# A decoder block on one core: constants loaded later, mixing moved a unit on, gates paired by branch, head outputs turned among the last row blocks

## The chip, the core and the metric

The kernel runs on one core of a Trainium2 chip. The metric is the device time of one execution in microseconds (us). An execution's time holds the span that the profile shows and what lies around it. TensorE (PE) multiplies matrices, VectorE (DVE) and ScalarE (ACT) work on elements, GpSimd (POOL) does small jobs, and SyncE (SP) issues most of the DMA transfers. Each engine works through its own list of instructions in order, and semaphores tell it when an operand is there.

## The reference

One layer of a decoder block in float32, on 1024 positions of width 1024. The parts that matter here:

```python
u = rms_norm(h, mix_pre_g)
z = jnp.einsum('bsd,de->bse', u, w_in)
p, q, k, v = z[..., :o1], z[..., o1:o2], z[..., o2:o3], z[..., o3:o4]
gate_a, gate_b = z[..., o4:o5], z[..., o5:]
ya = jnp.einsum('bsc,cd->bsd', pool_mixer(p, pool_mix, pool_scale), w_branch_a)
yb = jnp.einsum('bsc,cd->bsd', diff_attention(q, k, v, ...), w_branch_b)
m = jax.nn.sigmoid(gate_a) * ya + jax.nn.sigmoid(gate_b) * yb
h = h + rms_norm(jnp.einsum('bsd,de->bse', m, w_out), mix_post_g)
# then a SwiGLU FFN of 2816 hidden columns
```

The pooling mixer takes running means over windows of 2, 4, 8 and 16 positions, one window for each of four groups of 128 channels, subtracts the input, mixes each group by a 128x128 matrix (`pool_mix`) and scales the channels (`pool_scale`). Differential attention has four heads. A head computes two softmaxes over causal scores with a linear bias, and uses the first minus lambda times the second; lambda comes from four vectors of 64 (`lam_q1` to `lam_k2`). Each head's output rows are normed and scaled by `subln_g` and a constant.

## The kernel before

Every operand of a matmul is split into a rounded part (`_hi`) and a residual (`_lo`), and a product is three matmuls: hi x hi, lo x hi, hi x lo. ScalarE writes most rounded parts, VectorE subtracts them from the source for the residuals.

**Projection.** Two columns blocks of 128 of `w_in`, with all 1024 positions, form a unit. A unit (`unit`, which calls `seven_steps`) computes its 2x2 blocks by seven products of 12 matmuls each in place of eight, on sums of the input's quadrants (A11 to A22, S1 to S4, made by `half_sums` on VectorE) and of the weights' quadrants (T1 to T4, made in `weights`). `done` takes each finished block (e is the column block, t the half of the positions) to where it goes. The first two heads' q and k are computed without that scheme while the input is still being normed and turned, by the functions `first_pair` and `common`; their blocks are stored by `qk_done` (L312 is the residual of q). Then come units for heads 2 and 3, four units for v and the pooled channels (`vp_unit`; `pool` takes the running means and mixes), and eight units for the gates, the unit d holding column block d of both gates. `gate_done` applies the sigmoid on ScalarE (L571) and stores the block in DRAM (`sgd`). What `pool` has to do is put in a list, `later`, and done at the start of the next unit's code, behind the loading of its weights.

**Constants.** Pool scale (`psc`), the gain of the head norm (`sgc`) and the four lambda vectors (`lamt`, whose tile shows as sg in the profile) are cleared on POOL (L472) and loaded by SyncE (L587 to L590); VectorE reduces the vectors (L593), ScalarE scales the gain (L600). The order on each engine is not that of the source: a scheduler hoists instructions whose operands it holds to be ready, and so this group stands between the half sums of the input, ahead of head 1's last blocks.

**Attention.** A row block of 128 queries goes through `scores` (matmuls, L690 and L691; VectorE adds the bias and takes the row extreme, L694; ScalarE takes the exponential, L697), `transposes` (L718, with ScalarE and VectorE copies) and `values` (L732; then ScalarE L737, VectorE L738, and ScalarE's square sum for the norm, L128). `seq` lists the row blocks: head after head, in the order QORDER within each. Scores run four row blocks ahead of values. Between the steps a filler gives TensorE other matmuls, some for each step as PACES says: the end of the last gate unit, and then the first branch (`branch` with e = 0: pooled outputs times `w_branch_a`, times the gate loaded from `sgd`, into `ma`). After a head's last row block `head_norm` takes the norm on POOL (L124), and four steps later (LAG) VectorE scales the head's rows (L748).

**After attention.** All four heads' outputs `O` are turned, 32 transposes of 128x128 on TensorE into PSUM tiles oT (L810); ScalarE writes the rounded part OTh (L812), VectorE the residual OTl (L813). Then the second branch (e = 1) computes column blocks 0 to 7 for both halves of the positions, adds the first branch's, and the output projection and the FFN follow.

SBUF tiles come from two rings, `a8` (16 tiles of 8 KB a partition) and `b4` (14 of 4 KB); PSUM has two banks for each of `mm` and `fil` and two tiles of two banks, `pair`. A tile can be written only when the last reader of its place in the ring is through.

Of the kernel before, what the change touches and what calls it, by code (L numbers as in the profile page):

```python
# [11 lines left out]
F32R = mybir.dt.float32r  # L12
# [3 lines left out]
P = 128  # L16
# [16 lines left out]
QORDER = (7, 0, 6, 1, 5, 2, 4, 3)  # L33
LAG = 4
# [5 lines left out]
def block_kernel(ctx, tc, x, w_in, pool_mix, pool_scale, w_branch_a, lam_q1, lam_k1, lam_q2,  # L40
# [121 lines left out]
    def split(o, a):  # L162
        hi, lo = o
        nc.scalar.copy(hi, a)  # L164
        sub(lo, a, hi)
        return o
# [245 lines left out]
    with tc.manual_schedule(engines={nc.tensor.engine, nc.scalar.engine, nc.vector.engine, nc.gpsimd.engine}):  # L412
# [58 lines left out]
        for t in (psc, sgc, lamt):  # L471
            nc.gpsimd.memset(t, 0.0)  # L472
# [64 lines left out]
    def pool(g, p, s0):  # L537
# [17 lines left out]
        split(y, p)  # L555
        o = pair("y")
# [10 lines left out]
    def gate_done(d):  # L567
        st, seen = [b4([P, S], F32, "g_st") for _ in range(2)], [0, 0]

        def done(e, t, src):  # L570
            nc.scalar.activation(st[e][:, half(t)], src, AF.Sigmoid)  # L571
# [59 lines left out]
    for d in range(KD - 1):  # L631
        if d == 3:
            next(head0)
        unit(w_cols(o_ga, d), w_cols(o_gb, d), gate_done(d))

    last_unit = seven_steps(weights(w_cols(o_ga, KD - 1), w_cols(o_gb, KD - 1)), U, gate_done(KD - 1))
# [16 lines left out]
    def branch(e, w, mov, take):  # L653

        for d in range(KD):
            bh, bl = load_w(w[:, d * P:(d + 1) * P], 4, P, "wb", e == 0)
            for t in range(2):
                sg = temp(("p1", "sg")[t])
                nc.sync.dma_start(sg, sgd[e][d][:, half(t)])
                o = fil("branch")  # L660
                for k in range(4):
                    triple(o, bh[:, k, :], bl[:, k, :], *mov(t, k), k == 0, k == 3, False)
                    yield
                take(d, t, o, sg)
# [78 lines left out]
    def head_norm(h):  # L743
        r = rstd_of(oss[h], NB, P)
        defer(LAG, lambda: scale_head(h, r))

    def scale_head(h, r):
        nc.vector.tensor_tensor(out=O[h], in0=O[h], in1=r.unsqueeze(2).to_broadcast([P, NB, P]), op=ALU.mult)  # L748
# [15 lines left out]
    seq = [(h, qb) for h in range(NH) for qb in QORDER]  # L764
# [18 lines left out]
    for i in range(-AHEAD, len(seq)):  # L783
# [21 lines left out]
    OT = [(a8([P, 2, S], F32R, "OTh"), a8([P, 2, S], F32R, "OTl")) for _ in range(2)]  # L805
    for h in range(NH):
        for t in range(2):
            pt = mm("oT")
            for i in range(4):
                nc.tensor.transpose(pt[:, i * P:(i + 1) * P], O[h][:, t * 4 + i, :], ident)  # L810
            dh, dl = OT[h // 2][0][:, h % 2, half(t)], OT[h // 2][1][:, h % 2, half(t)]
            nc.scalar.mul(dh, pt, sgc)  # L812
            nc.vector.scalar_tensor_tensor(out=dl, in0=pt, scalar=sgc, in1=f32(dh), op0=ALU.mult,  # L813
                                           op1=ALU.subtract)

# [404 lines left out]
```

## Time and profile before

| | us |
|---|---|
| median of three runs | 1288.24 |
| fastest and slowest of the three | 1286.24, 1288.36 |
| profiled execution | 1285.73 |
| its span | 1283.9 |
| PE busy in the span | 1254.4 |
| DVE, ACT, POOL busy | 835.6, 583.3, 142.7 |

The span goes from the first to the last instruction of one execution; 1.8 us of that execution lie around it. Busy is the time in which an engine worked on at least one instruction. A row of the timeline gives start, duration, engine, line and operation, what is written and read, and in brackets how long the engine stood idle before it and what ended that. In the projection TensorE starts a matmul of 512 columns every 0.227 us. The projection takes the span up to about 350 us, attention goes from there to about 500, the second branch to 545, and the output projection and the FFN take the rest.

### The profile page before, as it was taken

The numbers are of one execution on the slowest core, as the hardware profiler recorded it, in microseconds if no ns is written. First come the engines' busy times: TensorE is split into PE (matmuls) and PEld (weight loads), VectorE is DVE, ScalarE is ACT, GpSimd is POOL, SyncE is SP. The second block draws the span as 40 slices with busy tenths as digits, with TensorE's granted clock in tenths as the row PEclk, the third lists the DMA queues.
The fourth block names the chain that finished last, engine by engine and source line by source line (L and its number), as shares of the span: only waits on it lengthen the run. The fifth ranks groups of instructions, "written<-read, shape, count | busy, mean of one in ns | idle before, by whom it ended". The sixth has DMA issues, their size and how long they took to land.

```text
span 1283.9 us, 15774 instructions
## 1 busy us (share of the span) xinstructions
PE 1254.4 (98%) x5912; PEld 1041.6 (81%) x5912; DVE 835.6 (65%) x1297; ACT 583.3 (45%) x1037; POOL 142.7 (11%) x131
## 2 busy tenths in 40 slices
PE   8899999999989998999999999999999999999997
PEld 8788778888778887878878888888888888888886
DVE  5785766345479997665599565556556537965666
ACT  7453344434586675244454333333333333554542
POOL 4100000000101100001102110111110111000221
PEclk9899999999999999999999999999999999999999
DMA  8254336233688412544224223233223268833235
GB/s 255 94 164 164 136 133 217 82 131 107 210 264 220 135 52 65 184 146 163 83 90 140 88 85 115 99 107 123 99 100 98 95 197 279 266 107 94 88 106 205
DMA packets 139788, 179.16 MB, mean 140 GB/s; under 512 B 8000, under 2 KB 94528, under 8 KB 137280
## 3 DMA queue, kind: packets, MB, share of 16 engines
q1 hardware_dynamic: 129024, 146.70, 36.5%
q10 hardware_dynamic: 10688, 31.46, 6.4%
q8 instruction: 46, 0.75, 0.3%
q14 instruction: 30, 0.25, 0.1%
HBM read 124.39 MB, written 53.74 MB: 139 GB/s over the span
## 4 chain that ended last, share of the span: by engine, by line
PE 81%; DVE 7%; DMA 4%; ACT 3%; issue 2%; POOL 2%; SPq 0%; ACTq 0%; DVEq 0%; POOLq 0%
PE Y L231 9%; PE Y L232 9%; PE Y L233 9%; PE X L231 5%; PE X L232 5%; PE X L233 5%; PE Yd L232 3%; PE Yd L233 3%; PE Yd L231 3%; PE Z L232 2%; PE Z L233 2%; PE Z L231 2%; PE o L732 2%; PE wo L873 2%; PE wo L874 2%
## 5 line engine op out<-in xcount | busy, mean ns | idle before, releaser
L160 DVE TENSOR_TENSOR p<-Z,p 128x512 f32<-128x512 f32 x35 | 24.2, 691 | 159.2 <-PE Z L233 155.6
L232 PE MATMUL Y<-A_lo,Wh 128*128 128x512 f32 x296 | 115.6, 391 | 0.3 <-DVE A_lo L87 0.3
L231 PE MATMUL Y<-A_hi,Wh 128*128 128x512 f32 x296 | 115.3, 390 | 0.0
L233 PE MATMUL Y<-A_hi,Wl 128*128 128x512 f32 x296 | 115.2, 389 | 0.0
L231 PE MATMUL Y<-S_hi,Wh 128*128 128x512 f32 x280 | 109.2, 390 | 0.0
L232 PE MATMUL Y<-S_lo,Wh 128*128 128x512 f32 x280 | 109.2, 390 | 0.0
L231 PE MATMUL X<-S_hi,Wh 128*128 128x512 f32 x280 | 109.1, 389 | 0.1
L233 PE MATMUL Y<-S_hi,Wl 128*128 128x512 f32 x280 | 109.1, 390 | 0.0
L233 PE MATMUL X<-S_hi,Wl 128*128 128x512 f32 x280 | 109.0, 389 | 0.0
L232 PE MATMUL X<-S_lo,Wh 128*128 128x512 f32 x280 | 109.0, 389 | 0.0
L200 ACT CAST Wh<-wf_t 128x1024 fp32r<-128x1024 f32 x70 | 72.8, 1053 | 71.8 <-PE X L232 30.6
L200 ACT CAST Wh<-w_raw 128x1024 fp32r<-128x1024 f32 x72 | 60.6, 843 | 65.6 <-PE Z L232 40.0
L87 DVE TENSOR_TENSOR w_op<-wd,w_op 128x512 fp32r<-128x512 f32 x77 | 56.3, 732 | 51.0 <-ACT w_op L164 51.0
L87 DVE TENSOR_TENSOR Wl<-wf_t,Wh 128x1024 fp32r<-128x1024 f32 x70 | 86.6, 1244 | 2.9 <-ACT Wh L200 2.9
L164 ACT CAST w_op<-wd 128x512 fp32r<-128x512 f32 x77 | 47.9, 622 | 74.6 <-PE Yd L233 31.3
L87 DVE TENSOR_TENSOR Wl<-w_raw,Wh 128x1024 fp32r<-128x1024 f32 x72 | 69.5, 966 | 14.0 <-ACT Wh L200 14.0
L232 PE MATMUL Yd<-w_op,s_op 128*128 128x512 f32 x176 | 68.7, 390 | 0.3 <-DVE w_op L87 0.2
L231 PE MATMUL Yd<-w_op,s_op 128*128 128x512 f32 x176 | 68.6, 390 | 0.0
L233 PE MATMUL Yd<-w_op,s_op 128*128 128x512 f32 x176 | 68.3, 389 | 0.0
L160 DVE TENSOR_TENSOR wf_t<-w_raw,wf_t 128x512 f32<-128x512 f32 x70 | 65.7, 938 | 1.0
L232 PEld LDWEIGHTS Y<-A_lo,Wh 128*128 128x128 f32 x296 | 55.6, 188 | 12.1 <-DVE A_lo L87 0.7
L231 PEld LDWEIGHTS Y<-A_hi,Wh 128*128 128x128 f32 x296 | 55.6, 188 | 11.5
(266 smaller groups left out, 3062.3 us busy)
## 6 DMA issues: line engine op xcount, KB each, us to landing
s_raw<-fsd SPq DMA_DIRECT2D x35, 512.0 KB, 3.6
w_raw<-in_w_in_dram SPq DMA_DIRECT2D x32, 512.0 KB, 4.2
w_raw<-in_w_ffn_gate_dram SPq DMA_DIRECT2D x22, 512.0 KB, 3.8
w_raw<-in_w_ffn_up_dram SPq DMA_DIRECT2D x22, 512.0 KB, 3.8
fsd<-fss SPq DMA_DIRECT2D x11, 1024.0 KB, 3.9
wd<-in_w_ffn_down_dram SPq DMA_DIRECT2D x44, 256.0 KB, 5.4
fsd<-F SPq DMA_DIRECT2D x33, 256.0 KB, 2.3
qkd<-qk_st ACTq DMA_DIRECT2D x16, 512.0 KB, 3.8
```

The costliest lines, as they stand in the source:

```text
L87: nc.vector.tensor_tensor(out=o, in0=a, in1=f32(hi), op=ALU.subtract)
L160: nc.vector.tensor_tensor(out=o, in0=a, in1=b, op=op)
L164: nc.scalar.copy(hi, a)
L200: nc.scalar.copy(hi, a)
L231: nc.tensor.matmul(o, ah, bh, start=start, stop=False, skip_group_check=goes_on)
L232: nc.tensor.matmul(o, ah, bl, start=False, stop=False, skip_group_check=goes_on)
L233: nc.tensor.matmul(o, al, bh, start=False, stop=stop, skip_group_check=goes_on)
L732: nc.tensor.matmul(o, ats[b // 4][:, j, b % 4 * P:(b % 4 + 1) * P], V[:, b, :, :], start=b == 0 and j == 0, stop=b == qb and j == 1)
L873: nc.tensor.matmul(o[e], mh[:, k, :], wl, start=False, stop=False)
L874: nc.tensor.matmul(o[e], ml[:, k, :], wh, start=False, stop=k == KD - 1)
```

## The change

Four things are changed.

1. The constants' tiles are cleared later: no longer by memsets after the first heads, but at head 3, by POOL copies that read head 2's q tile (the values are overwritten by the loads). The loads cannot come before.
2. `pool` ends with the split of its result; the mixing is a function of its own, `mix`, put in `later` for the unit after. `unit` does only what was in the list when it began.
3. The gate units hold two column blocks of the same gate: first gate a's blocks in pairs, then gate b's. Of the last pair, gate b's blocks 6 and 7, which are finished among the attention's first steps, the values are stored as they are, and the second branch applies the sigmoid when it has loaded them.
4. The last head's row blocks run from 7 to 0. Heads 0 to 2 are turned after its rows 7, 6 and 5 (`turn_head`, in a PSUM tile of `pair`), the upper half of head 3 is normed after row 4, the lower after row 0, and each is turned some steps later. The second branch takes the upper halves of column blocks 0 and 1 first.

```diff
+QLAST = (7, 6, 5, 4, 3, 2, 1, 0)
...
-        for t in (psc, sgc, lamt):
-            nc.gpsimd.memset(t, 0.0)
...
         split(y, p)
+        later.append(lambda: mix(g, pm, y))
+
+    def mix(g, pm, y):
         o = pair("y")
...
+    GATES = [(e, d) for e in range(2) for d in range(KD)]
+    gate_pairs = [GATES[i:i + 2] for i in range(0, 2 * KD, 2)]
+    unfinished = gate_pairs[-1]
...
-            nc.scalar.activation(st[e][:, half(t)], src, AF.Sigmoid)
+            if pair == unfinished:
+                nc.scalar.copy(st[e][:, half(t)], src)
+            else:
+                nc.scalar.activation(st[e][:, half(t)], src, AF.Sigmoid)
             seen[e] += 1
             if seen[e] == 2:
-                nc.scalar.dma_start(sgd[e][d], st[e])
+                b, d = pair[e]
+                nc.scalar.dma_start(sgd[b][d], st[e])
...
-        while later:
+        for _ in range(len(later)):
             later.pop(0)()
...
     for h in range(2, NH):
-        unit(w_cols(o_q, h), w_cols(o_k, h),
-             W=W if h == 2 else None, done=partial(qk_done, h, st=[a8([P, 2, S], F32R, "qk_st") for _ in range(2)]))
-
+        st = [a8([P, 2, S], F32R, "qk_st") for _ in range(2)]
+        if h == 3:
+
+            for t in (psc, sgc, lamt.rearrange("p i d -> p (i d)")):
+                nc.gpsimd.tensor_copy(t, f32(late[:, 0, :t.shape[-1]]))
+        late = st[0]
+        unit(w_cols(o_q, h), w_cols(o_k, h), W=W if h == 2 else None, done=partial(qk_done, h, st=st))
...
+        order = [(d, t) for d in range(KD) for t in range(2)]
+        if e == 1:
+            order[:4] = [(0, 1), (1, 1), (0, 0), (1, 0)]
...
+            if (e, d) in unfinished:
+                nc.scalar.activation(sg, sg, AF.Sigmoid)
...
+    def turn_head(h, t):
+
+        if len(OT) <= h // 2:
+            OT.append((a8([P, 2, S], F32R, "OTh"), a8([P, 2, S], F32R, "OTl")))
+        pt = pair("oT")[:, 0, :]
+        for i in range(4):
+            nc.tensor.transpose(pt[:, i * P:(i + 1) * P], O[h][:, t * 4 + i, :], ident)
+        dh, dl = OT[h // 2][0][:, h % 2, half(t)], OT[h // 2][1][:, h % 2, half(t)]
+        nc.scalar.mul(dh, pt, sgc)
+        nc.vector.scalar_tensor_tensor(out=dl, in0=pt, scalar=sgc, in1=f32(dh), op0=ALU.mult, op1=ALU.subtract)
...
-    seq = [(h, qb) for h in range(NH) for qb in QORDER]
+    seq = [(h, qb) for h in range(NH) for qb in (QLAST if h == NH - 1 else QORDER)]
...
-            if (i + 1) % len(QORDER) == 0:
-                head_norm(i // len(QORDER))
+            h, pos = divmod(i, len(QORDER))
+            if h < NH - 1 and pos == len(QORDER) - 1:
+                head_norm(h)
+            elif h == NH - 1 and pos < NH - 1:
+                for t in range(2):
+                    turn_head(pos, t)
+            elif h == NH - 1 and pos % 4 == 3:
+                b = slice(4, 8) if pos == 3 else slice(0, 4)
+                head_norm(h, b)
+                defer(LAG, partial(turn_head, h, b.start // 4))
...
-    for h in range(NH):
-        for t in range(2):
-            pt = mm("oT")
```

How this moves instructions on the engines is shown at three places. First VectorE, before, where the sums of the input's last quadrants end the first stage (A_raw and S_raw hold the sums, A_lo the residuals, sg_153 the lambda vectors, lsum their products' sums, qk_st head 1's q and k):

```order
L160 TENSOR_TENSOR S_raw_93<-S_raw_93,S_raw_94 128x4x128
L593 ISA sg_153,lsum_1054<-sg_153 128x64
L593 ISA lsum_1054 128x1
L160 TENSOR_TENSOR A_raw_91<-S_raw_93,A_raw_91 128x4x128
L160 TENSOR_TENSOR S_raw_94<-S_raw_94,A_raw_91 128x4x128
L160 TENSOR_TENSOR A_raw_92<-A_raw_92,A_raw_91 128x4x128
L312 SCALAR_TENSOR_TENSOR qk_st_575<-q_154,qk_st_575 128x512
L87 TENSOR_TENSOR qk_st_578<-k_155,qk_st_578 128x512
```

Of the change, the place where the same reduction (now L611) stands, in the unit of head 2 (p_141 and u_142 take its blocks, Y_801 and X_803 are its products; Wl and wf_t are weights of the unit behind head 3):

```order
L161 TENSOR_TENSOR p_141_830<-Y_801,p_141_830 128x512
L611 ISA sg_153,lsum_1054<-sg_153 128x64
L611 ISA lsum_1054 128x1
L88 TENSOR_TENSOR Wl_1079<-w_raw_1074,Wh_1078 128x1024
L88 TENSOR_TENSOR qk_st_800<-p_141_830,qk_st_800 128x512
L161 TENSOR_TENSOR u_142_844<-X_803,u_142_844 128x512
L611 ISA sg_153,lsum_1054<-sg_153 128x64
L611 ISA lsum_1054 128x1
L88 TENSOR_TENSOR Wl_1087<-wf_t_1082,Wh_1086 128x1024
```

The first reduction moved from between the sums of the first stage to some 40 rows later on VectorE; the three sums now follow each other directly.

Second, ScalarE at the start of attention, before (E is a row block's scores, nm their row extremes, g_st a gate's blocks, AT the transposed weights of attention):

```order
L697 ACT_TABLE_LOAD
L697 ACTIVATE E_2743,sums_2746<-E_2743,nm_2745 128x1024
L697 ACTIVATE E_2744,sums_2746<-E_2744,nm_2745 128x1024
L571 ACT_TABLE_LOAD
L571 ACTIVATE g_st_2706<-p_464_2754 128x512
L697 ACT_TABLE_LOAD
L697 ACTIVATE E_2788,sums_2790<-E_2788,nm_2789 128x128 x2
L697 ACTIVATE E_2831,sums_2834<-E_2831,nm_2833 128x896
L571 ACT_TABLE_LOAD
L571 ACTIVATE g_st_2707<-p_468_2780 128x512
L697 ACT_TABLE_LOAD
L697 ACTIVATE E_2832,sums_2834<-E_2832,nm_2833 128x896
```

The same place of the change:

```order
L722 ACT_TABLE_LOAD
L722 ACTIVATE E_2743,sums_2746<-E_2743,nm_2745 128x1024
L722 ACTIVATE E_2744,sums_2746<-E_2744,nm_2745 128x1024
L582 COPY g_st_2706<-p_464_2754 128x512
L722 ACTIVATE E_2788,sums_2790<-E_2788,nm_2789 128x128 x2
L722 ACTIVATE E_2831,sums_2834<-E_2831,nm_2833 128x896
L582 COPY g_st_2707<-p_468_2780 128x512
L722 ACTIVATE E_2832,sums_2834<-E_2832,nm_2833 128x896
L582 COPY g_st_2707<-u_474_2807 128x512
```

The sigmoids became copies, and the table loads between them and the exponentials are gone, but for the first.

Third, TensorE at the end of attention, before (o is a row block's output before the norm, O the outputs of heads 0 to 3 as O_2735 to O_2738, branch the second branch's sums):

```order
L718 MATMUL aT_4535<-ident,E_4427 128x128 x4
L732 MATMUL o_4543<-V_3720,AT_4514 128x256 x8
L732 MATMUL o_4543<-V_3720,AT_4519 128x256 x2
L732 MATMUL o_4564<-V_3720,AT_4540 128x256 x8
L810 MATMUL oT_4641<-ident,O_2735 128x128 x4
L810 MATMUL oT_4648<-ident,O_2735 128x128 x4
L231 MATMUL branch_4705<-OTh_4637,wb_hi_4698 128x512
L810 MATMUL oT_4655<-ident,O_2736 128x128 x4
L232 MATMUL branch_4705<-OTl_4638,wb_hi_4698 128x512
```

Of the change, the turning of head 1 among the scores of the last head (branch is still the first branch, the filler):

```order
L715 MATMUL s_4371<-K_3710,QA_3709 128x384
L716 MATMUL s_4371<-K_3710,QB_3719 128x384
L232 MATMUL branch_4657<-y2h_2982,wb_hi_4650 128x512
L789 MATMUL oT_4419<-ident,O_2736 128x128 x4
L233 MATMUL branch_4657<-y2l_2983,wb_hi_4650 128x512
L234 MATMUL branch_4657<-y2h_2982,wb_lo_4651 128x512
L232 MATMUL branch_4657<-y2h_2982,wb_hi_4650 128x512
L789 MATMUL oT_4426<-ident,O_2736 128x128 x4
L233 MATMUL branch_4657<-y2l_2983,wb_hi_4650 128x512
L757 MATMUL o_4401<-V_3720,AT_4309 128x256 x8
```

and the last row blocks of the change, with the filler's last matmuls and the first of the second branch:

```order
L232 MATMUL branch_4673<-y2h_2982,wb_hi_4650 128x512
L789 MATMUL oT_4591<-ident,O_2738 128x128 x4
L757 MATMUL o_4598<-V_3720,AT_4567 128x256 x6
L743 MATMUL aT_4615<-ident,E_4512 128x128
L233 MATMUL branch_4673<-y2l_2983,wb_hi_4650 128x512
L234 MATMUL branch_4673<-y2h_2982,wb_lo_4651 128x512
L232 MATMUL branch_4710<-OTh_4347,wb_hi_4703 128x512
L233 MATMUL branch_4710<-OTl_4348,wb_hi_4703 128x512
L234 MATMUL branch_4710<-OTh_4347,wb_lo_4704 128x512
L757 MATMUL o_4620<-V_3720,AT_4588 128x256 x4
L757 MATMUL o_4628<-V_3720,AT_4617 128x256 x2
```

Of the eight turns, six moved up among the last head's row blocks and one stands among its last; the one left, of head 3's lower half, comes 16 matmuls of the second branch behind the last row block. The filler ends among the last row blocks instead of ahead of them.

More of the change, by code (lines that the diff above doesn't have):

```diff
@@ L630, in block_kernel @@
     head0 = load_head(0)
-    for d in range(KD - 1):
-        if d == 3:
+    for i, pair_cols in enumerate(gate_pairs[:-1]):
+        if i == 3:
             next(head0)
-        unit(w_cols(o_ga, d), w_cols(o_gb, d), gate_done(d))
-    last_unit = seven_steps(weights(w_cols(o_ga, KD - 1), w_cols(o_gb, KD - 1)), U, gate_done(KD - 1))
+        unit(*gate_cols(pair_cols), gate_done(pair_cols))
+    last_unit = seven_steps(weights(*gate_cols(unfinished)), U, gate_done(unfinished))
     for _ in range(4):
@@ L653, in branch @@
     def branch(e, w, mov, take):
-        for d in range(KD):
-            bh, bl = load_w(w[:, d * P:(d + 1) * P], 4, P, "wb", e == 0)
-            for t in range(2):
[L658 to L664, printed above, removed]
+        order = [(d, t) for d in range(KD) for t in range(2)]
+        if e == 1:
+            order[:4] = [(0, 1), (1, 1), (0, 0), (1, 0)]
+        ws = {}
+        for d, t in order:
+            if d not in ws:
+                ws[d] = load_w(w[:, d * P:(d + 1) * P], 4, P, "wb", e == 0)
+            bh, bl = ws[d]
+            sg = temp(("p1", "sg")[t])
+            nc.sync.dma_start(sg, sgd[e][d][:, half(t)])
+            if (e, d) in unfinished:
+                nc.scalar.activation(sg, sg, AF.Sigmoid)
+            o = fil("branch")
+            for k in range(4):
+                triple(o, bh[:, k, :], bl[:, k, :], *mov(t, k), k == 0, k == 3, False)
+                yield
+            take(d, t, o, sg)
     ma = []
@@ L741, in values, with head_norm, scale @@
         yield
[L743 to L748, printed above, removed]
+    OT = []
+    def head_norm(h, b=slice(0, NB)):
+        n = b.stop - b.start
+        r = rstd_of(oss[h][:, b], n, P)
+        def scale():
+            o = O[h][:, b, :]
+            nc.vector.tensor_tensor(out=o, in0=o, in1=r.unsqueeze(2).to_broadcast([P, n, P]), op=ALU.mult)
+        if h < NH - 1:
+            defer(LAG, scale)
+        else:
+            scale()
+    def turn_head(h, t):
[7 more added lines that the diff above has]
+        nc.vector.scalar_tensor_tensor(out=dl, in0=pt, scalar=sgc, in1=f32(dh), op0=ALU.mult, op1=ALU.subtract)
     y2 = []
```

12 lines of the change are left out of this document (3 added, 9 removed).

## The prediction

> **What bounds the kernel now.** The page comes first, then busy time by stretches of 20 us, then what TensorE waits for.
>
> ```profile
> PE 1254.4 (98%) x5912; PEld 1041.6 (81%) x5912; DVE 835.6 (65%) x1297; ACT 583.3 (45%) x1037; POOL 142.7 (11%) x131
> ```
>
> TensorE is the bound: 1283.9 - 1254.4 leaves 29.5 us of idle span. The diff neither adds nor removes a matmul, so the change can only win idle time or clock. Where they lie:
>
> ```profile
> 40.00:60.00 20.00, 16.73 (x84) 14.39 (x84) 14.14 (x19) 7.97 (x11) 0.00 (x0) 0.83 0.42 136
> 360.00:380.00 20.00, 16.18 (x95) 12.94 (x93) 14.57 (x40) 17.66 (x40) 1.98 (x1) 1.00 0.88 279
> 380.00:400.00 20.00, 19.56 (x116) 17.18 (x117) 18.69 (x48) 13.71 (x39) 1.28 (x1) 1.00 0.88 228
> 460.00:480.00 20.00, 20.00 (x128) 17.86 (x127) 18.26 (x50) 13.82 (x41) 2.93 (x2) 1.00 0.14 42
> 480.00:500.00 20.00, 17.32 (x113) 14.60 (x112) 14.17 (x35) 12.81 (x37) 1.64 (x1) 1.00 0.21 66
> 500.00:520.00 20.00, 19.28 (x90) 14.73 (x89) 14.19 (x21) 5.12 (x8) 0.00 (x0) 1.00 0.30 93
> ```
>
> After the span's bounds come busy us of PE, PEld, DVE, ACT, POOL, then granted clock, DMA share and GB/s. Idle sits at 40 to 60 (3.27, and the only clock below 1), at attention's start (3.82 and 0.44) and its end (2.68 and 0.72). Who ends it:
>
> ```profile
> PE q L106 <- DVE qk_st L312: 3.3, 1, 3.3
> PE s L690 <- DVE nm L694: 3.0, 5, 1.0
> PE o L732 <- DVE O L738: 1.5, 3, 0.5
> PE aT L718 <- DVE O L738: 1.4, 3, 0.5
> PE o L732 <- DVE AT L87: 1.2, 2, 0.6
> PE y L106 <- ACT yh L164: 1.0, 2, 0.7
> PE aT L718 <- DVE AT L87: 0.9, 2, 0.5
> PE oT L810 <- DVE OTl L813: 0.9, 2, 0.6
> ```
>
> (us, times, longest.) One wait of 3.3 us in the projection, two for the mixing, the rest in attention. That is all that the change's four parts can reach.
>
> **Constants.** The chain at 40 us, in time order:
>
> ```profile
> 43.04 0.20 ACT L600 ACTIVATE sgc<-sgc 128x1 f32<-128x1 f32 x1 [4.02 <-DMA sgc<-in_subln_g_dram]
> 45.78 0.22 DVE L593 CUSTOM_DVE_ANT_0 sg<-sg 128x64 f32<-128x64 f32 x1 [4.84 <-DMA sg<-in_lam_k_dram]
> 48.23 0.68 DVE L312 SCALAR_TENSOR_TENSOR qk_st<-q,qk_st 128x512 fp32r<-128x512 f32 x1
> 48.97 0.80 PE L106 MATMUL q<-A_hi,w_hi 128*128 128x512 f32 x1 [3.27 <-DVE qk_st L312]
> 50.19 0.43 PE q L108
> 55.10 0.23 PE q L108
> ```
>
> VectorE stands 4.84 us on a load of the lambda vectors, ScalarE 4.02 on that of the gain; four additions and conversions later TensorE, idle since 48.97 - 3.27 = 45.70, goes on. Its matmuls then follow each other by 0.43 us until 54.5, and by 0.23 after. The change takes these two operations out of the place: VectorE starts its three sums at 45.78 - 4.84 = 40.9, ScalarE is free from 39.0, and head 1's q residual (0.68) is done at about 44.2, ahead of 45.70. Gain: 3.27 of idle, and (54.5 - 48.97) / 0.43 = 13 matmuls x (0.43 - 0.23) = 2.6 of clock: **5.9**.
>
> [...]
>
> What is late next: the constants now wait for head 2's first q half on ScalarE, are cleared by three POOL copies in place of memsets, and then pass SyncE, which has three weight loads ahead of them and the rest behind.
>
> ```profile
> 83.82 0.64 ACT L311 ACTIVATE qk_st<-p 128x512 fp32r<-128x512 f32 x1
> 90.36 0.69 DVE L160 TENSOR_TENSOR p<-Y,p 128x512 f32<-128x512 f32 x1 [1.03 <-PE Y L233]
> 103.73 0.69 DVE L160 TENSOR_TENSOR p<-Z,p 128x512 f32<-128x512 f32 x1 [3.50 <-PE Z L233]
> sg<-in_lam_q_dram SPq DMA_DIRECT2D x2, 32.0 KB, 5.2
> 37.62 1.23 DVE L160 TENSOR_TENSOR A_raw<-A_raw,A_raw 128x512 f32<-128x512 f32 x1
> 33.27 0.69 DVE L160 TENSOR_TENSOR A_raw<-S_raw,A_raw 128x512 f32<-128x512 f32 x1
> ```
>
> In before's clock: q half done 84.5, about 1 us of copies (estimate: the memset's 0.5 to 2), four issues of some 0.5, landing 5.2 later: 92.6. VectorE reaches the reduction at 91.05, after the sum of row 90.36: a wait of 0 to 2.5 us, taken as 1.5. Behind it stand a residual of the weights of the unit after head 3 and head 2's k residual; head 3's unit, 7 products x 12 matmuls x 0.23 = 19 us, has its weights already, and VectorE idles 3.50 in it. So it costs TensorE **0**, and at most 2.5 if that cover were gone. [...]
>
> **Mixing.** Six matmuls wait 1.0 us in all for their ScalarE conversion; a unit (19 us) later it is long done. Gain **1.0**. Three tiles are held a unit longer out of 14; bounds 0 to 1.0.
>
> **Gates.** ScalarE in attention's start:
>
> ```profile
> 355.15 1.28 ACT L571 ACT_TABLE_LOAD   x1
> 356.44 0.63 ACT L571 ACTIVATE g_st<-p 128x512 f32<-128x512 f32 x1
> ...
> L571 ACT ACT_TABLE_LOAD x5 | 6.4, 1283 | 0.1
> ```
>
> Four gate pieces stand among the exponentials. Each loads its table and then has the exponentials load theirs: eight loads, of the five in the row and as many of L697's. 8 x 1.28 = 10.3 us of a ScalarE that is busy 17.66 of 20. The pieces become copies of like length (0.6), so rows of scores leave ScalarE up to 10 us earlier, and the filler, which is the end of the last unit, is spread otherwise. TensorE can win at most its idle of 3.82 + 0.44 = 4.3. VectorE's own 18.69 of 20 and the loads at a share of 0.88 come next, so I take somewhat over half: **2.5** (0 to 4.3). [...] The four sigmoids and one load return in the second branch, 4 x 0.63 + 1.28 = 3.8 us on a ScalarE that is busy 5.12 of 20 from 500 on: **0**; up to 3.8 if the output weights' conversion behind them were late.
>
> **Last head.** Rows of the old end:
>
> ```profile
> 486.37 0.39 PE L233 MATMUL branch<-y2h,wb_lo 128*128 128x512 f32 x1
> L812 ACT ACTIVATE OTh<-oT,sgc 128x512 fp32r<-128x512 f32 x8 | 5.5, 689 | 4.0 <-PE oT L810 3.9
> L813 DVE SCALAR_TENSOR_TENSOR OTl<-oT,sgc,OTh 128x512 fp32r<-128x512 f32 x8 | 5.9, 749 | 2.3 <-ACT OTh L812 2.2
> L737 ACT ACTIVATE O<-o,rec 128x128 f32<-128x128 f32 x32 | 11.5, 360 | 17.6 <-PE o L732 17.6
> L738 DVE SCALAR_TENSOR_TENSOR O<-o,rec,O 128x128 f32<-128x128 f32 x32 | 11.1, 345 | 5.0 <-ACT O L737 5.0
> L128 ACT ACTIVATE junk<-O 128x128 bf16<-128x128 f32 x32 | 9.8, 307 | 10.7 <-DVE O L738 10.7
> L748 DVE TENSOR_TENSOR O<-O,rstd 128x1024 f32<-128x1024 f32 x4 | 5.9, 1468 | 0.8 <-POOL rstd L124 0.8
> 498.08 1.64 POOL L124 TENSOR_TENSOR rstd<-ms,mhalf 128x8 f32<-128x8 f32 x1 [25.18 <-DVE ms L123]
> 488.08 1.70 PE L732 MATMUL o<-V,AT 128*128 128x256 f32 x12 [0.52 <-DVE O L738]
> 501.69 0.66 PE L810 MATMUL oT<-ident,O 128*128 128x128 f32 x4 [0.64 <-DVE OTl L813]
> ```
>
> The filler's last matmul is that of 486.37, and from 488.08 to 501.69 seven waits of 0.26 to 0.64 add up to 2.68 + 0.72 = 3.4 us. Now six of eight turns (0.69 on ScalarE, 0.75 on VectorE) are done in the head's upper rows, beside scores, and the rows that come last are the short ones, with the filler's last matmuls between them. From the reordered last rows, head 3's lower half is normed through ScalarE 0.36, VectorE 0.35, ScalarE 0.31, POOL (half of 1.64 to all of it) and VectorE (half of 1.47), 2.6 to 3.4 without hand-overs, while 16 branch matmuls of 0.23 give 3.7 of cover. Against that, VectorE, 18.26 of 20 busy at 460 to 480, takes 6 x 0.75 = 4.5 more there. I take half of the idle, **1.7**, less 1.0 of new waits; bounds -4.5 (all of VectorE's added work shows) to 3.4.
>
> Sum: 5.9 + 1.0 + 2.5 + 1.7 - 1.0 = 10.1. The profiled execution, 1285.73 with a span of 1283.9, would be 1275.6. It lies 2.5 below the median of the runs shown, 1288.24; from that I predict **1278**.
>
> **Rivals.** (A) Attention gives its share back: VectorE becomes the bound of the last head and the first rows, so that 2.5 + 0.7 vanish: 1288.2 - 6.9 = 1281.3. For it: 18.26 and 18.69 of 20. Against it: in the same stretches TensorE is busy 20.00 and 19.56, so VectorE hardly holds it now. (B) All of the idle in attention goes: 6.9 + 4.3 + 3.4 = 14.6, 1273.6. Against it: the waits on VectorE's row maxima, 3.0 us, lie on a chain that the change doesn't shorten. (C) Slower: the turns use the two PSUM pairs that the scores use. A pair is held through transpose, ScalarE and VectorE, 0.66 + 0.69 + 0.75 = 2.1; if TensorE stands all of that at eight turns, 16.8 is lost against 9.4 won elsewhere, near 1296. It decides from (9.4 + 2.6) / 8 = 1.5 us a turn. Against it: filler matmuls and a second pair stand between. (D) The change doesn't do what it says at the start: the wait moves to the reduction of head 2 in full, or another operand holds the residual past 45.70, so that 3.27 and the clock stay; alone it gives 10.1 - 5.9 = 4.2, 1284; with A it is 1.0, 1287.2. (E) The half clock of 48.97 to 54.5 was not in the runs that make the median: 10.1 - 2.6 = 7.5, 1280.7. Against it: the profiled execution, which has it, is no slower than the three runs.
>
> **Numbers.** Forecast 0.43, A 0.20, B 0.12, C 0.07, D alone 0.05, D with A 0.06, E 0.07. What this kernel's measurement can tell from no change is about 0.2%, 2.6 us. Faster by more holds the forecast, A, B, E and D alone, 0.87; I keep 0.86; same 0.07, slower 0.07. The range takes in B with 1.6 below it for the runs' own spread of 2.1 us, and D alone with 1 above: 1272 to 1285, leaving out C and D with A, 0.13.
>
> **What would show it.** Right: clock 1.00 and PE above 19.5 of 20 in the stretch at 40; no ScalarE table load among the first exponentials; no wait of the mixing; TensorE's waits in attention, 8.9 us in the list above, down to about 6. Wrong: a wait of TensorE on the reduction or on the weights of the unit after head 3, near 90 to 110; scores waiting for a turn's residual; the output projection waiting for its converted weights behind a sigmoid; VectorE over 19 of 20 in the last head with TensorE below 19.

## The result, and the profile after

| | before | changed |
|---|---|---|
| median of five runs, us | 1288.24 | 1274.49 |
| fastest and slowest | 1286.24, 1290.49 | 1272.09, 1274.83 |
| profiled execution, its span | 1285.73, 1283.9 | 1272.09, 1270.3 |
| PE busy | 1254.4 | 1248.5 |

The ratio is 0.989, with a 95% interval from 0.9874 to 0.9906: some 14 us, 12 to 16. The changed kernel was timed again later, beside other kernels on one chip, at 0.9908 [0.9893, 0.9923], some 12 us. The forecast was 10 us; the time lies in the range and near the rival B, though B's reason is not what happened.

The page of the changed kernel, and its busy time by stretches (columns as before: PE, PEld, DVE, ACT, POOL, granted clock, DMA share, GB/s):

```profile
PE 1248.5 (98%) x5912; PEld 1039.5 (82%) x5912; DVE 837.6 (66%) x1299; ACT 576.1 (45%) x1034; POOL 143.4 (11%) x132
```

```profile
40.00:60.00 20.00, 20.00 (x112) 17.48 (x111) 17.92 (x21) 9.83 (x12) 0.00 (x0) 1.00 0.36 128
...
360.00:380.00 20.00, 17.34 (x97) 13.81 (x97) 16.32 (x45) 12.09 (x37) 1.28 (x1) 1.00 0.70 211
380.00:400.00 20.00, 19.94 (x127) 17.52 (x127) 18.56 (x45) 13.12 (x39) 2.95 (x2) 1.00 1.01 250
...
460.00:480.00 20.00, 20.00 (x140) 17.98 (x139) 18.42 (x47) 13.71 (x40) 1.64 (x1) 1.00 0.13 41
480.00:500.00 20.00, 19.50 (x108) 16.11 (x107) 14.59 (x35) 9.28 (x29) 2.01 (x2) 1.00 0.28 89
500.00:520.00 20.00, 20.00 (x90) 16.57 (x89) 12.40 (x19) 4.42 (x6) 0.00 (x0) 1.00 0.51 161
```

What TensorE still waits for in the stages of the change (us, times, longest):

```profile
PE s L715 <- DVE nm L719: 3.1, 4, 1.2
...
PE s L716 <- DMA QB<-qkd: 1.1, 1, 1.1
...
PE wo L915 <- DVE wol L88: 0.9, 2, 0.6
PE o L757 <- DVE O L763: 0.6, 1, 0.6
PE oT L789 <- DVE O L776: 0.5, 1, 0.5
```

The stretch at 40 is full and at full clock. The waits for head 1's q and for the mixing are gone, of those at the end of attention one of 0.5 is left, and the waits for the row extremes (nm) stay as they were, 3.1 us. Idle is down by 29.5 - 21.8 = 7.7, but the span by 13.6. The rest, 5.9, is in the busy time of TensorE; 2.8 of it is the half clock behind the wait at 48 us, as is worked out below. So idle alone does not tell what a wait costs.

A better measure is the distance between marks, the starts of matmuls that both programs have, in the traces: the first Z matmul of head 2's unit, that of a gate unit (at 227.14 before, 218.53 after), head 0's first QB matmul, the output projection's first matmul, and the last group of turns ahead of the FFN.

| us | start to Z | Z to gates | gates to QB | QB to output projection | to last turns | rest |
|---|---|---|---|---|---|---|
| before | 76.27 | 150.87 | 114.37 | 204.36 | 105.42 | 632.6 |
| changed | 69.86 | 148.67 | 115.02 | 198.18 | 105.92 | 632.7 |
| difference | -6.41 | -2.20 | +0.65 | -6.18 | +0.50 | 0 |

The first column holds the constants, the second the mixing, the fourth the gates' and the last head's parts with the second branch. The third is longer since the first scores wait 1.07 for their QB load, 0.42 before; with any one part alone it is longer too, by 0.5 to 1.1, so this is not the work of one part.

### The profile page after: what moved, and what is told of

It reads as the page before. It is cut to its first block, busy times and chain, and to the rows that moved or that the text cites. A ratio compares the mean times of both kernels' runs of the same rounds, so it can differ in the third digit from the quotient of the medians.

```text
span 1270.3 us, 15788 instructions
## 1 busy us (share of the span) xinstructions
PE 1248.5 (98%) x5912; PEld 1039.5 (82%) x5912; DVE 837.6 (66%) x1299; ACT 576.1 (45%) x1034; POOL 143.4 (11%) x132
## 4 chain that ended last, share of the span: by engine, by line
PE 86%; DVE 5%; DMA 3%; ACT 3%; issue 1%; POOL 1%; SPq 0%; DVEq 0%; POOLq 0%; ACTq 0%
PE Y L234 10%; PE Y L233 10%; PE Y L232 10%; PE X L234 5%; PE X L232 5%; PE X L233 5%; PE Z L234 3%; PE Yd L233 3%; PE Z L233 3%; PE Yd L234 3%; PE Z L232 3%; PE Yd L232 3%; PE wo L915 2%; PE wo L916 2%; PE o L757 2%; PE wo L914 2%
## 5 line engine op out<-in xcount | busy, mean ns | idle before, releaser
L234 PEld LDWEIGHTS Y<-A_hi,Wl 128*128 128x128 f32 x296 | 55.6, 188 | 11.5
```

What stands on the lines that cost most here:

```text
L234: nc.tensor.matmul(o, al, bh, start=False, stop=stop, skip_group_check=goes_on)
```

## The experiments

Twelve runs. Each kernel was timed beside the kernel before on its chip. All ratios are of it.

**One part alone.** Four kernels, each the kernel before with one part of the change's diff. The main lines of each part:

```diff
const:  -        for t in (psc, sgc, lamt):
        -            nc.gpsimd.memset(t, 0.0)
        +            for t in (psc, sgc, lamt.rearrange("p i d -> p (i d)")):
        +                nc.gpsimd.tensor_copy(t, f32(late[:, 0, :t.shape[-1]]))
mix:    +        later.append(lambda: mix(g, pm, y))
gate:   +    gate_pairs = [GATES[i:i + 2] for i in range(0, 2 * KD, 2)]
        +            if (e, d) in unfinished:
        +                nc.scalar.activation(sg, sg, AF.Sigmoid)
tail:   +QLAST = (7, 6, 5, 4, 3, 2, 1, 0)
        +                    turn_head(pos, t)
        +            order[:4] = [(0, 1), (1, 1), (0, 0), (1, 0)]
```

> The kernel before with the constants' part alone. Theory 1 (the parts add up, and a wait of TensorE costs more than the idle that the profile gives it, by the tail of the last matmul and the slow start of the next, some 0.27 us a wait): the first transposes of v start 6.4 us earlier than before's 123.6, the lead stays at 6.4 to the end, near 1281.8 against 1288.2. Theory 2 (idle as recorded, plus the half clock): a lead of 5.9, 1282.3. Theory 3 (the lead is lost again in attention, where loads or VectorE set the pace): 6.4 at the transposes, under 4 at the first matmul of the output projection.

> The kernel before with the mixing a unit later, and nothing else. Theory 1: the two waits of 1.0 us cost with their tails and slow starts near 2.2 us; the gates' units start 2.2 us earlier, and the end is 2.2 earlier, near 1286.0. Theory 2 (idle as recorded): 1.0 to 1.1, 1287.1. Theory 3: it only pays together with the others, since without the constants' part the order around the mixing is another: under 0.5.

> The kernel before with the gates paired by branch and the last pair's sigmoid in the second branch, and nothing else. Theory 1: the eight table loads hold the rows of the first head up; without them TensorE's idle at attention's start falls from 4.3 to about 2.7 and with fewer waits some 2 us are won, near 1286.2. Theory 2: the idle moves to other waits of the same rows (VectorE's row extremes, the loads), under 0.7 us won, 1287.6 or more. In both the sigmoids in the second branch cost nothing: the time from the second branch's first matmul to the output projection's stays within 0.3 us of before's.

> The kernel before with the last head's order, the turning among its rows and the second branch's order, and nothing else. Theory 1: seven waits of 3.4 us in all fall to about one, and with their tails and slow starts 4.0 to 4.5 are won, near 1284. Theory 2 (idle as recorded): 2.9, 1285.3. Theory 3 (VectorE, with 4.5 us more among the rows of the last head, gives it back): under 1.5, with TensorE's idle in the last head's rows up by 2.

| | ratio | start to Z | Z to gates | gates to QB | QB to output projection | to last turns | half-clock stretches |
|---|---|---|---|---|---|---|---|
| before | 1 | 76.27 | 150.87 | 114.37 | 204.36 | 105.42 | two windows at 48 |
| const | 0.9965 [0.9952, 0.9978] | 69.72 | 150.88 | 114.98 | 204.24 | 106.57 | none |
| mix | 0.9994 [0.9985, 1.0004] | 74.77 | 148.65 | 115.11 | 204.28 | 106.86 | one at 48 |
| gate | 0.9988 [0.9978, 0.9997] | 75.86 | 150.83 | 115.49 | 203.50 | 106.13 | two at 48, one at 385 |
| tail | 0.9980 [0.9970, 0.9990] | 75.09 | 150.89 | 114.91 | 202.08 | 107.86 | one at 48, one in 540 to 560 |

Each part wins in its own stage. The constants win 6.55 at Z in the trace, the lead of theory 1, and 4.5 us (1286.85 x 0.0035) in time. Theory 1 had the lead stay to the end; in the trace it is 6.05 at the output projection's first matmul and 4.9 at the last turns. The mixing wins 2.22 between Z and the gates and nothing behind them (that its Z comes earlier is one half-clock window less at 48, which the edit does not touch). That is theory 1 by the trace; the time, between 0.5 slower and 1.9 faster, doesn't tell it from no change and lies below theory 1's 2.2. For the other two theory 1 asked for 2 and 4 to 4.5; the stage shows 0.9 and 2.3, the time 1.5 and 2.6. The last head's part is thus nearest to its theory 2, 2.9.

The sigmoids in the second branch cost nothing, though the stretch that was to show it, from that branch's first matmul to the output projection's, grew by 0.8 (48.62 to 49.40) and not by at most 0.3. The turns lie in that stretch; from the last of them on it is 40.66 us in both.

The gates' 0.9 is too little for the idle that went, and the trace says why. Windows and timeline of the gates' kernel (in the timeline: start, duration, engine, line and operation, idle before and releaser):

```profile
380.00:400.00 20.00, 17.78 (x96) 15.02 (x95) 15.22 (x42) 11.84 (x34) 0.04 (x1) 0.91 0.70 172
```

```profile
382.65 0.33 PE L703 MATMUL s<-K,QA 128*128 128x128 f32 x1 [0.89 <-DVE nm L707]
...
384.65 0.47 PE L703 MATMUL s<-K,QA 128*128 128x448 f32 x1 [1.19 <-DVE nm L707]
...
386.39 0.63 PE L233 MATMUL branch<-y2h,wb_lo 128*128 128x512 f32 x1
386.82 0.63 PE L231 MATMUL branch<-y2h,wb_hi 128*128 128x512 f32 x1
...
389.56 0.40 PE L232 MATMUL branch<-y2l,wb_hi 128*128 128x512 f32 x1
389.79 0.40 PE L233 MATMUL branch<-y2h,wb_lo 128*128 128x512 f32 x1
```

From 385.6 to 389.0, 3.4 us, matmuls start 0.43 apart in place of 0.23, behind two waits of 0.89 and 1.19 with small matmuls between them. That is a second half-clock episode, of half the length of that at 48, and it costs half of 3.4, 1.7 us. The changed kernel has the same two waits (0.89 at 373.99, 1.19 at 375.98) and keeps its clock; the last section sets the two beside each other. Less 1.7 the gates' stage would be 201.8, a gain of 2.6.

Only part of this gain lies at attention's start. In the stage's first 80 us recorded idle falls from 4.36 to 2.90. Another 1.3 falls at the old end: the waits that the prediction finds there add up to 3.4, in the gates' kernel to 2.15. Before, the filler's last matmul starts at 486.37, and the last row blocks' value matmuls go on without it until 495.59. In the gates' kernel the filler lasts until they are through:

```profile
492.18 2.42 PE L745 MATMUL o<-V,AT 128*128 128x256 f32 x18
494.44 0.39 PE L233 MATMUL branch<-y2h,wb_lo 128*128 128x512 f32 x1
```

Why it ends later there is not shown.

**Both attention parts, each taken out.** The changed kernel without the last head's part (notail) and without the gates' part (nogate), their diffs the change's own, reversed.

> The changed kernel without the last head's part (old order of its row blocks, the turning and the second branch as before). Between attention's first QB matmul and the output projection's first the change alone saved 6.2 us of before's 204.4, while at full clock the gates alone saved some 2.5 (0.8 as recorded, with 3.4 us of half clock in it) and the last head's part alone 2.3. Theory A (the parts add up, and the rest is chance in where the half clock falls): this kernel saves 2 to 3 there. Theory B (the gates' gain is larger behind the other parts, or the last head's part needs it): it saves 0.8 or less, or 4. Up to the first QB matmul it is like the changed kernel: 8.0 us ahead of before.

> The changed kernel without the gates' part (a unit holds both gates' same column block, sigmoids among the first exponentials). Theory A (parts add): between the first QB matmul and the output projection 2 to 3.5 us less than before's 204.4. Theory B (the two attention parts need each other): about as the last head's part alone, 2.2, and the rest of the 6.2 shows only with both.

| | ratio | start to Z | Z to gates | QB to output projection | half clock there |
|---|---|---|---|---|---|
| notail | 0.9938 [0.9922, 0.9953] | 70.06 | 148.68 | 201.87 | none |
| nogate | 0.9935 [0.9920, 0.9951] | 69.90 | 148.68 | 203.38 | one window at 420 to 440 |
| changed, again | 0.9908 [0.9893, 0.9923] | 70.02 | 148.61 | 198.15 | none |

The gates alone are worth 2.5 in the stage (204.36 - 201.87). The last head's part is worth 2.3 alone and, nogate less a window's 1.7, some 2.7. Together they are worth 6.2, so that 1.0 to 1.4 come only with both. Theory A holds for most of it and not for all. The traces show where the two meet: of the 3.4 us of idle at the old end some 2.1 are left with either part alone, and 0.5 with both. The times point the same way, 3.9 and 3.5 us lost by taking the last head's or the gates' part out against 2.6 and 1.5 won by each alone, but intervals of 1 to 3 us on each are too wide to show it.

**The half clock by itself.** The kernel before, with work for TensorE in the place of its 3.3 us of idle.

```diff
         first_pair(3, 1)
+        pt = pair("warm")[:, 0, :]
+        for i in range(28):
+            nc.tensor.transpose(pt[:, i % 4 * P:(i % 4 + 1) * P], ident, ident)
```

> The kernel before with 28 more transposes of the identity on TensorE just ahead of the matmul that waits 3.3 us for head 1's q; their results are not used. The loads and VectorE's wait stay. Theory H (idle in TensorE makes the half clock): the granted clock is 1.00 in the stretch from 40 to 60, matmuls behind the wait follow each other by 0.23 from the first, and the first unit's Z matmuls start some 2.6 to 3 us ahead of before's 76.27, near 73.5; the other 3.5 of the constants' part stays. Theory L (the half clock has another cause than TensorE's idle): the drop stays, and Z starts at 75 to 76.3. In time H gives -2.6 at most where the drop has two windows, -1.5 where it has one.

Windows and timeline of this kernel:

```profile
40.00:60.00 20.00, 20.00 (x126) 17.99 (x125) 14.66 (x22) 7.99 (x12) 0.00 (x0) 1.00 0.41 135
```

```profile
45.30 3.22 PE L485 MATMUL warm<-ident 128*128 128x128 f32 x28
48.28 0.47 PE L106 MATMUL q<-A_hi,w_hi 128*128 128x512 f32 x1
48.59 0.39 PE L107 MATMUL q<-A_lo,w_hi 128*128 128x512 f32 x1
48.81 0.39 PE L108 MATMUL q<-A_hi,w_lo 128*128 128x512 f32 x1
```

Theory H in the trace: the clock stays at 1.00 and the matmuls follow each other by 0.23 but for the first (0.31). The waiting matmul starts 0.69 earlier than before (48.28), since VectorE's wait for the load ended 0.8 earlier here, and Z at 73.07, 3.20 earlier: 2.5 are the clock. Kernel const, at 69.72, lies another 3.35 ahead; 48.28 - 45.30 = 2.98 of it is the wait that this kernel still has. In time the 3.2 don't show: the ratio is 1.0000 [0.9992, 1.0009], where theory H asked for 1.5 to 2.6 us. The clock is higher in its other runs too, 0.9982 on average over twelve against 0.9965 over the seventeen of before, so they lose as much elsewhere. In its trace the stage of the output projection is 108.80, 3.4 longer than before's, with waits of 0.6 to 1.2 for its weights and a half-clock window at 540 to 560; the mixing lost 0.8 more. This one execution shows where its own time went; that all executions lose it there is not shown.

**The turns among the rows.** The changed kernel with heads 0 to 2 turned behind the last rows, everything else kept.

```diff
-        if len(OT) <= h // 2:
+        while len(OT) <= h // 2:
...
-            elif h == NH - 1 and pos < NH - 1:
-                for t in range(2):
-                    turn_head(pos, t)
...
     for _ in filler:
         pass
+    for h in range(NH - 1):
+        for t in range(2):
+            turn_head(h, t)
```

> The changed kernel with heads 0 to 2 turned behind the last rows, ahead of the second branch, in place of among the last head's upper rows; the descending order of the last rows, the halves of head 3's norm and the second branch's order stay. Theory T (turning among the rows is what pays): the turns again wait for each other's conversions, six of them with 1 to 2 us of idle and their tails: 2 to 3 us slower than the changed kernel, all of it between the last row block and the second branch. Theory Q (the descending order is what pays, since short rows leave the filler among them): within 1 us of the changed kernel.

Ratio 0.9929 [0.9916, 0.9941], 3.7 us over the changed kernel beside it (1277.84 to 1274.13), somewhat more than theory T's 2 to 3. The stage is 202.95, with a half-clock window at 360 to 380 in it: 201.2, 3.1 longer. TensorE at the end of its attention, three of its four waits there, 2.4 us in all:

```profile
488.55 0.73 PE L232 MATMUL branch<-OTh,wb_hi 128*128 128x512 f32 x2 [0.82 <-ACT OTh L791]
490.02 0.63 PE L789 MATMUL oT<-ident,O 128*128 128x128 f32 x4 [0.28 <-DVE ms L124]
492.48 0.66 PE L789 MATMUL oT<-ident,O 128*128 128x128 f32 x4 [0.56 <-DVE OTl L792]
```

and of the changed kernel, where one wait, 0.5, is left in this place:

```profile
484.96 0.66 PE L789 MATMUL oT<-ident,O 128*128 128x128 f32 x4 [0.50 <-DVE O L776]
```

Theory T: turning among the rows is what pays. Whether it would pay in the old order of the rows was not tried.

**Three tries to win more.** The changed kernel with two steps more of the last gate unit ahead of the first scores, with more filler in the second ten steps, and with both.

```diff
lead6:  -    for _ in range(4):
        +    for _ in range(6):
                 next(last_unit)
pace:   -PACES = (2.2, 0.5, 0.3, 0.3)
        +PACES = (2.2, 0.8, 0.3, 0.3)
v1:     both
```

> The changed kernel with six steps of the last gate unit in place of four ahead of the first scores, and the filler's second pace 0.8 in place of 0.5. The first covers the 1.1 us that TensorE waits for head 0's q residuals, the second puts filler between the scores that wait 0.9 and 1.2 for VectorE some 40 us later. Expected from theory 1: 1.1 + 2.1 of idle with tails less what is missing of the filler at the end, 1 to 3 us faster than the changed kernel; its rival: the idle comes back where the filler ends, within 0.5 us.

> The changed kernel with six steps of the last gate unit ahead of the first scores in place of four, the filler's paces as they are. Theory 1: the 1.1 us wait for head 0's q residuals goes (stretch up to the first QB matmul 0.8 shorter, as in the run with both edits), and attention stays within 0.5 us: about 1 us faster than the changed kernel. Theory 2: the filler, two steps shorter, moves against the rows of scores, and the 4.4 us that the run with both edits lost between QB and the output projection come from this edit: 3 us slower.

> The changed kernel with the filler's second pace 0.8 in place of 0.5, and nothing else. If theory 1 of the lead-of-six kernel holds, this edit is what lost 4.4 us in attention: 3 to 4 us slower than the changed kernel, with the idle between 400 and 470 us at 3.5 to 4 in place of 1.5. If not, within 1 us.

> The changed kernel once more, to have it beside the others on one chip. Expected 0.989 of before. The trace should repeat the distances between marks that hold no loads to 0.1 us (first unit's Z to the gates' 148.67 us), and differ by up to 2 us in attention and the output projection, where loads and half-clock windows fall otherwise.

| | ratio | gates to QB | QB to output projection |
|---|---|---|---|
| changed, again | 0.9908 [0.9893, 0.9923] | 114.98 | 198.15 |
| lead6 | 0.9909 [0.9895, 0.9922] | 114.68 | 199.44 |
| pace | 0.9932 [0.9920, 0.9945] | 114.44 | 201.96 |
| v1 | 0.9930 [0.9915, 0.9945] | 114.23 | 202.60 |

None beats the changed kernel, so theory 1 of v1 and of lead6 fell. The two extra steps shorten the way to QB by 0.3, not 0.8, and lengthen attention by 1.3, and the time is the same. The pace costs 3.8 in attention and 3.7 in time: of the two edits in v1, this is the one that lost. Its idle in the stage is 8.5 us where the changed kernel has 4.9; half of the difference lies in these stretches, where the changed kernel has PE at 19.97 and 18.45:

```profile
400.00:420.00 20.00, 19.20 (x119) 16.65 (x119) 17.09 (x45) 13.34 (x38) 0.00 (x0) 1.00 0.92 255
420.00:440.00 20.00, 17.31 (x107) 14.64 (x108) 17.88 (x47) 13.17 (x42) 4.91 (x3) 1.00 0.16 50
```

The repetition of the changed kernel gave the same distances within 0.2 us, except the output projection's (106.17 for 105.92, within 0.3): its own traces differ by little.

## Why the prediction was right, step by step

**Constants: forecast 5.9, measured 6.4.** The chain was read right, and its two terms nearly. Before, the matmul ahead of the wait:

```profile
45.41 0.28 PE L108 MATMUL k<-A_hi,w_lo 128*128 128x256 f32 x1
```

Such matmuls follow each other by 0.12, so the one of 48.97 could have started at 45.53: the wait cost 3.44 (3.27 forecast). From it to Z before takes 27.30, the changed kernel from its own such matmul (45.35) 24.51: the half clock cost 2.8 (2.6 forecast; filling the idle showed 2.5). The remaining 0.18 is an earlier start of the changed kernel's trace. Its timeline at the two places, the old and the new:

```profile
42.73 0.68 DVE L313 SCALAR_TENSOR_TENSOR qk_st<-q,qk_st 128x512 fp32r<-128x512 f32 x1
...
84.83 0.23 DVE L611 CUSTOM_DVE_ANT_0 sg<-sg 128x64 f32<-128x64 f32 x1 [0.16 <-DMA sg<-in_lam_k_dram]
```

```profile
45.23 0.28 PE L109 MATMUL k<-A_hi,w_lo 128*128 128x256 f32 x1
45.35 0.40 PE L107 MATMUL q<-A_hi,w_hi 128*128 128x512 f32 x1
```

```profile
78.11 0.71 POOL L602 COPY psc<-qk_st 128x4 f32<-128x4 f32 x1 [39.99 <-ACT qk_st L312]
78.77 0.66 POOL L602 COPY sgc<-qk_st 128x1 f32<-128x1 f32 x1
79.36 1.62 POOL L602 COPY sg<-qk_st 128x512 f32<-128x512 f32 x1
```

The residual ends at 43.4, 2 us ahead of TensorE. Where the loads went, VectorE waits 0.16 (1.5 forecast), though the three POOL copies take 3.0 us, three times the estimate: landing took less than the 5.2 of before (the issue of 81.41 and the wait's end at 84.83 are 3.4 apart). Beside the third copy one sum on VectorE, at 80.43, took 1.10, its like at 82.05 took 0.68, 0.4 less; before, the sums of 37.62 and 33.27 took 1.23 and 0.69. What made the longer ones longer is not shown. TensorE has no wait there, as forecast; rival D fell.

**Mixing: forecast 1.0, measured 2.2 in its stage** (in the time of the part alone, 0.8, it can't be told from nothing). The mechanism is right, the size is not. The step that took recorded idle for cost is what failed. Before, at the first of the two waits:

```profile
140.00 0.60 PE L527 MATMUL vT<-ident,p 128*128 128x128 f32 x4
141.29 0.50 PE L106 MATMUL y<-yh,pm 128*128 128x512 f32 x1 [0.69 <-ACT yh L164]
141.63 0.39 PE L231 MATMUL X<-S_hi,Wh 128*128 128x512 f32 x1
```

Elsewhere in the trace the next matmul starts 0.35 to 0.36 after the first of four such transposes (once 0.41), so y could have started at 140.36 and started 0.93 later; the profile counts idle only from the modelled end of the last transpose, 0.69. Then the matmul after the wait needs 0.34 to the next start in place of 0.23. So this one wait costs 1.04. The second, recorded as 0.33 ahead of 182.65, costs 0.6 by the same reckoning. A third place, at 188.76, where the next matmul came 0.71 after the first of four transposes and took 0.34 to the next, costs 0.46 and isn't in the list of waits at all. That is 2.1 of the 2.2, where recorded idle gives 1.0.

**Attention: forecast 2.5 + 1.7 - 1.0 = 3.2, measured 6.2, less 0.65 ahead of it.** Of the step on the gates the size was right for the part alone (2.5 forecast, 2.5 and 2.6 shown), in part by luck: of the idle at attention's start, from which it was taken, 1.5 went, and 1.3 went at the old end, which the step left out. One table load is left among the first exponentials, and the sigmoids in the second branch stood under cover. ScalarE in the changed kernel:

```profile
L722 ACT ACT_TABLE_LOAD x1 | 1.3, 1283 | 0.0
```

```profile
516.28 1.28 ACT L684 ACT_TABLE_LOAD   x1 [0.28 <-DMA p<-sgd]
517.58 0.63 ACT L684 ACTIVATE p<-p 128x512 f32<-128x512 f32 x1
519.04 0.63 ACT L684 ACTIVATE sg<-sg 128x512 f32<-128x512 f32 x1 [0.83 <-DVE m L161]
520.54 1.05 ACT L874 CAST woh<-wo_raw 128x1024 fp32r<-128x1024 f32 x1 [0.87 <-DMA wo_raw<-in_w_out_dram]
```

The output weights' conversion behind them waits for its own load, not for a sigmoid.

Two steps on the last head failed. "I take half of the idle": of 3.4 in the old end 0.5 is left, one wait of seven. For this part alone half was not far off (2.1 left); there the filler ends at 483.86, 18 us ahead of the last row's values. The rest went only with the gates' part, with which the filler lasts until the last rows; the prediction put that down to their new order. And "less 1.0 of new waits", from VectorE's 4.5 us more of work: VectorE is at 18.42 of 20 in the stretch at 460, where the six turns now are, hardly above before's 18.26, with TensorE at 20.00. The turns' work left a place where TensorE waited for it. So rival A fell, and C with it: turns cost TensorE no wait for a pair of PSUM banks that the waits list shows. Rival B gave nearly the right time by a wrong sum: recorded idle in attention fell by 4, from 10.0 to 6.0 with the wait for QB ahead of the stage, and not to nothing; 1.5 of the stage's 6.2 was never recorded as idle. That the waits which went took this unrecorded share with them, as in the mixing, is argued and not shown one by one. With the gates' part alone it is the other way: 3.0 of recorded idle went, and the stage won 2.5 at full clock.

**E.** The half clock falls otherwise in other executions: two windows at 48 us in two of the profiled executions that still have the wait, one window in two others. But the distance of median from profile, 2.5 before and 2.4 after, was carried over rightly, by some luck: later medians of before, over 9 to 29 runs, are 1286.39 to 1286.90, only 0.7 to 1.2 above its profile. What share of the median the clock makes isn't known from these runs; the rival's time, 1280.7, is well above the measured one.

**What stays open.** The four parts alone give 4.5, 0.8, 1.5 and 2.6 in time, 9.4 in all, against 12 to 14 together, with intervals of 1 to 2 us on each. Their stages give 6.6, 2.2, 0.9 (2.6 at full clock) and 2.3. The traces of the single parts lose 0.7 to 2.4 in the output projection and up to 1.4 behind it against before's trace. In the output projection TensorE waits 0.7 us for its weights in before's trace and 1.1 to 2.0 in these four; whether that is chance, or a kernel with fewer parts loses there as a rule, wasn't tried. Part of it is which execution was profiled: before's profile lies 0.7 to 1.2 below the later medians, those of the gates' and the last head's kernels 2.4 and 2.5 above their own.

## What to carry to other kernels

Where one engine is the bound, measure a wait by start-to-start distances around it, or by the distance between two marks that both programs have, not by the idle that the profile records: the mixing's short waits cost twice of it (2.1 us for 1.0), and one was not listed, while the gates' part won less than the idle that it removed (2.5 us for 3.0). A small load in VectorE's queue ahead of TensorE's next operand stopped TensorE here for most of VectorE's wait (4.8 us on VectorE, 3.4 on TensorE) and cost the clock besides (2.8); put such a load where the bound engine has a unit of work in store (TensorE then waited 0 on it here). Work of a helper engine at the tail of a stage was cheaper here, by 3.1 us, among the rows just ahead, even where that engine looks full (VectorE 18.42 of 20), with filler for the bound engine beside it. Before two such changes are priced apart, see where the filler ends with each: how it is dealt out is tuned to the rows, and more of it early cost 3.8 us later.

## What the runs showed of the hardware

The half clock came in windows of 3.4 us. In before it lasts from 47.88 to 54.70, two of them, in the gates' kernel from 385.6 to 389.0, one. In before it began 2.2 us into the wait of 3.27, not behind it. Two waits of 0.89 and 1.19 with small matmuls between them brought it in the gates' kernel and in the one with the turns behind the last rows (there the waits end at 373.59 and 375.58, and matmuls of 512 columns start 0.43 apart from 376.80 on), and in the changed kernel the same waits did not. As far as these traces show, it is where they fall that decides. In before's trace the clock changes at 47.88, 54.70 and 1280.09, and the 6.83 and 1225.39 us between are 2 and 359 times 3.413. Cut into such windows from its own drop, the gates' kernel has (columns as above)

```profile
382.17:385.58 3.41, 1.70 (x8) 1.31 (x9) 2.54 (x9) 2.42 (x7) 0.00 (x0) 1.00 0.00 0
385.58:388.99 3.41, 3.41 (x10) 2.75 (x9) 3.41 (x10) 0.49 (x2) 0.00 (x0) 0.50 0.79 229
```

and the changed kernel, cut back from its only change, at 1265.96, so that the grid lies otherwise against the same waits,

```profile
371.67:375.08 3.41, 2.20 (x12) 1.45 (x11) 2.06 (x4) 3.00 (x8) 0.00 (x0) 1.00 0.04 11
375.08:378.49 3.41, 2.51 (x11) 2.16 (x12) 3.21 (x9) 1.74 (x8) 0.00 (x0) 1.00 0.20 63
```

TensorE is idle 1.7 us in the window ahead of the drop, and 1.2 and 0.9 in the two that keep the clock. In before the window ahead of the drop, 44.46 to 47.87, has 2.2 us of idle. Of the windows of before and of the changed kernel that keep the clock, none has more than 1.6, the last 20 us of the program left out. Whether 1.7 us of idle in a window always bring the drop is not shown. The runs of one kernel show what this makes of times. Four of the gates' kernel's twelve, time and mean clock:

```
1282.19 us at 0.998   1284.39 us at 0.997   1286.34 us at 0.995   1289.37 us at 0.993
```

From 0.998 to 0.993 the clock withheld 0.005 x 1285 = 6.4 us, and the times differ by 7.2. The tie is not always so close: the twelve runs of the kernel with the 28 transposes differ by 2.9 us between clocks of 0.997 and 0.999, and one at 0.998 is the slowest. That a kernel with fewer waits has fewer windows that can fall so fits the changed kernel's five runs, at 0.997 to 0.999, beside 0.995 to 0.999 of before, and is not shown by itself.
